# An encoder layer in f32 on one core: token halves at the turns, weight casts tied to the put-backs, a 128-row rotary key, and feed-forward parts of 14 and 8 column groups

## The chip, the cores and the metric

The kernel runs on one core of a Trainium2 chip, in one launch. The metric is device time in microseconds (us). Before the change three runs gave 1837.91, 1840.97 and 1841.42 us; the median is 1840.97 us. The profiled execution took 1839.86 us, of which the profile's span covers 1838.1 us.

## The reference

One layer over 256 tokens of width 2048, everything in f32. `_modulate` shifts and scales by vectors that come from the conditioning vector c through `w_ada`, a 2048 x 18432 matrix.

```python
h = x + 0.5 * g1 * swiglu1(modulate(rms(x), c))       # D_FF = 5632
n = modulate(rms(h), c)
u, v, c_q, c_kv, k_pe = split(n @ w_in)
A = gelu(u) * spatial_gate(rms(gelu(v)))              # 8 channel groups, chunks of 128 tokens
B = latent_attention(c_q, c_kv, k_pe)                 # 8 heads; scores = q_nope.k_nope + q_pe.k_pe
h = h + g2 * (concat(rms(A), rms(B)) @ w_out)
h = h + 0.5 * g3 * swiglu2(modulate(rms(h), c))
out = rms(h)

def swiglu(x): return (silu(x @ w_gate) * (x @ w_up)) @ w_down
```

## The kernel before

**Products.** Every f32 product is made of three. `split` (L163) loads 1 MB of a weight into `raw`, ACT casts it in two pieces to a high part `whi` (L170), and DVE subtracts for the low part `wlo` (L174). The activations have high and low parts as well (`nh`, `nl`). PE adds nh·whi, nl·whi and nh·wlo in one PSUM bank: 24 matmuls of 128x512 for four rows of 128 of the contraction (k-tiles) and both halves of 128 tokens (t = 0, 1). `raw` has five buffers, which the columns of `w_ada` share; the split parts have room for two loads.

**Feed-forward.** `ffn` has 22 column groups; a group holds 256 columns of the gate and the same 256 of the up product, in one bank for each token half. The first FIRST = 12 groups are made with the contraction in parts: in the first feed-forward five parts of 3, 3, 3, 3 and 4 k-tiles (`grouped`), in the second three passes (`in_passes`). All groups go through part one, then all through part two, and so on. Between two parts the partial sums of a group leave PSUM: `keep_part` copies them to SBUF (L362), and `take_part` puts them back into a pair of banks before the group's next part (L366), both on ACT. After its last part a group goes through `swiglu` (tanh `th` on ACT at L326, products on DVE), and four transposes on PE (`tps`) with a cast on ACT (L350) make the input `s` of the down product. Then come the down product of these groups, the other ten groups (`rest`) and their down product, column by column c = 0 to 3 of 512, each followed by `add_out`, which multiplies by the gate row and adds to `h`.

**Order of the work.** Each engine runs its instructions in one order, fixed when the program is built; the program is written so that the load, cast and put-back of the next step (`begin` in `run`) stand behind the matmuls of the present step. In `begin`, `take_part` stands ahead of `load`, but nothing ties the two: the builder may place a load's casts ahead of the put-back copies on ACT if they are ready earlier.

**Turns.** Where a residual ends, `TokenNorm.add` squares each column of h on ACT, `done` reduces and takes the root for both halves together (the power on POOL, L182), with small matmuls `idle` on PE meanwhile (`keep_warm`), and `make` scales 256 columns of h (`hn`), flips them on PE (`tpn`) and writes the next `nh` and `nl`. After the second feed-forward the same norm with a gain gives the output, written by column in four transfers.

**Attention.** `scores` adds a 128-row product (kT, queries) and a 64-row product (kpeT, rotary queries) for each head and token half: the heads come in pairs, of which one uses rows 0 to 63 of the rotary tiles and one rows 64 to 127.

Of the kernel before, what the change touches and what calls it, by code (L numbers as in the profile page):

```python
# [17 lines left out]
P = 128  # L18
D = 2048
# [4 lines left out]
FIRST = 12  # L24
# [3 lines left out]
ADA_UP1 = (2, 2, 3, 2, 2, 3, 2, 2, 3, 2)  # L28
ADA_DOWN1 = ((0, 0, 0, 0, 1, 0), (1, 1, 1, 0, 0))
# [41 lines left out]
def encoder_layer(ctx: ExitStack, tc: tile.TileContext, outx, *, xT, x, pos, cst, vnorm, w_ada, gu1k, gu1, dn1a,  # L71
# [171 lines left out]
    class TokenNorm:  # L243


        def __init__(self):
            self.ss = stat(8)

        def add(self, c):
            for t in range(2):  # L250
                sq = tmp.tile([P, 512], F32, tag="hn", bufs=2, name="sq")
                act.activation(sq, h[:, t, c * 512 : c * 512 + 512], AF.Square, scale=1.0 / math.sqrt(D),
                               accum_out=self.ss[:, t * 4 + c : t * 4 + c + 1])

        def done(self, warm=False):
            ss = stat(2)
            if warm:
                keep_warm(mark["gu"], 6)
            dve.tensor_reduce(ss, self.ss.rearrange("p (t c) -> p t c", t=2), axis=AX.X, op=ALU.add)
            if warm:  # L260
                idle = bank("aux", "idle")
                keep_warm(mm(idle[:, :2], ident, ss, True, True), 6)
            self.r = rstd(ss, 2)

        def make(self, n, d0, sh, gs):
            hn = tmp.tile([P, 2, T], F32, tag="hn", bufs=2, name="hn")
            for t in range(2):
                dve.tensor_scalar(hn[:, t], h[:, t, d0 * P : d0 * P + T], self.r[:, t : t + 1], None, op0=ALU.mult)
            ps = bank("aux", "tpn")
            flip4(ps, lambda j, t: hn[:, t, j * P : j * P + P])  # L270
            for j in range(2):
                d = d0 + j
                nr = tmp.tile([P, T], F32, tag="nr", name="nr")
                s, g = mods[:, sh, d : d + 1], mods[:, gs, d : d + 1]
                o = ps[:, j * T : j * T + T]
                act.activation(n[0][:, d], o, AF.Identity, bias=s, scale=g)
                dve.tensor_scalar(nr, o, g, s, op0=ALU.mult, op1=ALU.add)  # L277
                dve.tensor_tensor(n[1][:, d], nr, n[0][:, d].bitcast(F32), op=ALU.subtract)  # L278

    def gate_row(m, c, g):  # L280

        ps = bank("aux", "tpg")
        flip4(ps, lambda j, t: mods[:, m, 4 * c + 2 * j + t : 4 * c + 2 * j + t + 1].to_broadcast([P, P]))
        act.copy(g, ps)

    def add_out(banks, c, g, norm=None):
        sl = slice(c * 512, c * 512 + 512)
        for t in range(2):
            e = tmp.tile([P, 512], F32, tag="hn", bufs=2, name="e")
            dve.tensor_tensor(e, banks[t], g, op=ALU.mult)  # L290
            dve.tensor_tensor(h[:, t, sl], h[:, t, sl], e, op=ALU.add)
        if norm:
            norm.add(c)
# [10 lines left out]
    def wide(w, banks, xs, first, last):  # L304

        half = (len(xs) + 1) // 2
        for i, ((whi, wlo), x) in enumerate(zip(w, (xs[:half], xs[half:]))):
            hi, lo = (y.rearrange("p (k c) -> p k c", k=len(x)) for y in (whi, wlo))
            for k, (a, b) in enumerate(x):
                for t in range(2):  # L310
                    mm(banks[t], a[:, token(t)], hi[:, k], first and i == 0 and k == 0, False)
                    mm(banks[t], b[:, token(t)], hi[:, k], False, False)
            for k, (a, _) in enumerate(x):
                for t in range(2):
# [3 lines left out]
    def gu_chunk(w, banks, n, kt0, nk, first, last):  # L318
        wide(w, banks, [(n[0][:, kt], n[1][:, kt]) for kt in range(kt0, kt0 + nk)], first, last)
# [11 lines left out]
    def ffn(gu, dn, n, gate, ada_pg, ada_dn, lead, groups, prep, norm, before_down=None):  # L331
        with tc.tile_pool(name="actp", bufs=1) as actp, tc.tile_pool(name="ftmp", bufs=2) as ftmp:
# [3 lines left out]
            grow = ftmp.tile([P, 4, 512], F32, bufs=1, name="grow")  # L336
# [27 lines left out]
            def take_part(part, pg, banks):  # L364
                for t in range(2):
                    act.copy(banks[t], part[pg][:, t])  # L366

            def run(steps, part, slots):


                def begin(pg, kt0, nk, opens, load, more):
                    new = banks
                    if opens and kt0:
                        new = [bank(tag(pg), "gu") for _ in range(2)]
                        take_part(part, pg, new)
                    w = load()
# [6 lines left out]
                for i, (pg, kt0, nk, opens, load, more) in enumerate(steps):  # L383
                    gu_chunk(w, banks, n, kt0, nk, kt0 == 0, kt0 + nk == KT)
# [10 lines left out]
            def in_passes(slots):  # L395
                def load(pg, kg):
# [4 lines left out]
                     for kgs in PASSES for pg in range(FIRST) for kg in kgs], {}, slots)  # L401
# [48 lines left out]
            for half in range(2):  # L450
# [5 lines left out]
                kqs = len(slots) // 4  # L456
                for c in range(4):
                    banks = [bank("acc" if c % 2 else "aux", "dn") for _ in range(2)]
                    for kq in range(kqs):
                        if half == 0 and before_down:  # L460
# [3 lines left out]
                        wide(w, banks, slots[kq * 4 : kq * 4 + 4], kq == 0, kq == kqs - 1)  # L464
                        turn()
                        if half == 0 and kq == 4:
                            gate_row(gate, c, grow[:, c])
                    add_out(banks, c, grow[:, c], norm if half else None)
# [59 lines left out]
    rb1 = tmp.tile([P, T], F32, bufs=1, name="rb1")  # L528
# [50 lines left out]
    ffn(gu1, (dn1a, dn1b), n1, G1, ADA_UP1, ADA_DOWN1, gu1k, [gu1g[f"gu1_{g}"] for g in range(len(GROUPS))], prep1, norm, gate_cols(G1))  # L579
# [3 lines left out]
    norm2.done(True)  # L583
    n2 = new_n()
    with tc.tile_pool(name="mix", bufs=1) as mix:
        u = mix.tile([P, 2, 1024], F32, name="u")
        vg = mix.tile([P, 2, 1024], F32, name="vg")
        cqT = mix.tile([P, 2, 4, T], F32R, tag="cm", name="cqT")
        ckvT = [mix.tile([P, 2, T], F32R, tag="qT", bufs=2, name="ckvT") for _ in range(2)]
        kpeT = mix.tile([P, T], F32, name="kpeT")  # L590
# [6 lines left out]
        def a_form(w, banks, lhs, kts, first, last):  # L597
            per = len(kts) // 2
            for half in range(2):
                hi, lo = (x.rearrange("p (k c) -> p k c", k=per) for x in w[half])  # L600
                ks = kts[half * per : half * per + per]
                for i, kt in enumerate(ks):
                    for t in range(2):
# [3 lines left out]
                for i, kt in enumerate(ks):  # L607
                    for t in range(2):
# [3 lines left out]
        def proj(i, kg, banks, n_ada, prep=False):  # L612
            if prep:
                for d in (kg * 4, kg * 4 + 2):
                    norm2.make(n2, d, SH2, SC2)
            w = split(win_a[i, kg])
            ada(n_ada)
            a_form(w, banks, n2, list(range(kg * 4, kg * 4 + 4)), kg == 0, kg == 3)
# [18 lines left out]
        def rotate(dst, x, heads):  # L637
# [3 lines left out]
            ps = tmp.tile([P, 4, 64 * heads], F32, tag="hn", bufs=2, name="ps")  # L641
            p1, p2, p3, p4 = (ps[:, i].rearrange("p (t a b) -> p t a b", t=2, a=heads) for i in range(4))
# [57 lines left out]
        for kg in range(4):  # L700
            proj(1, kg, banks, ADA_MIX["v0"][kg])
            if kg == 1:
# [3 lines left out]
                act.copy(kpeT, ps[:, :T])  # L706
# [154 lines left out]
        def a_flip():  # L861
            mA = nslot.tile([P, KT, T], F32R, tag="nl", name="mA")
            transpose_split(u, 8, (mA[:, :8], mA[:, 8:]), "out_norm_gmlp")
            return mA
# [5 lines left out]
        def scores(g, j):  # L870
            rows = slice(64 * j, 64 * j + 64)
            qt, qrt = qT[g]
            sc = bank("aux", "sc")
            for t in range(2):
                o = sc[:, t * T : t * T + T]
                mm(o, qt[:, j, t * P : t * P + P], kT[:, g * 2 + j], True, False)
                mm(o, qrt[rows, t * P : t * P + P], kpeT[rows], False, True)
# [28 lines left out]
        def out_pair(part, i, m, norm=None):  # L906
# [3 lines left out]
            if kq == 0:  # L910
                held[0] = [bank("acc", "wo") for _ in range(2)]
                held[1] = mix.tile([P, 512], F32, tag="grow", name="grow")
                gate_row(G2, c, held[1])
            ks = range(kq * 4, kq * 4 + 4)
            wide(w, held[0], [(m[:, k], m[:, 8 + k]) for k in ks], kq == 0, kq == 1)
            if kq:
                add_out(held[0], c, held[1], norm)
# [32 lines left out]
        mM = nslot.tile([P, KT, T], F32R, tag="nh", name="mM")  # L950
        for k in range(8):
# [3 lines left out]
            act.activation(mM[:, k], hr, AF.Identity, scale=g)  # L955
            dve.scalar_tensor_tensor(mM[:, 8 + k], hr, g, mM[:, k].bitcast(F32), op0=ALU.mult, op1=ALU.subtract)
        out_pair(0, 6, mA)
        out_pair(0, 7, mA)
        norm = TokenNorm()
        for dp in range(8):  # L960
# [5 lines left out]
    norm3.done(True)  # L966
    n3 = new_n()
# [8 lines left out]
    def prep3(kg, pg):  # L976
        if pg == 0 and kg < cut:
            for d in (kg * 4, kg * 4 + 2):
                norm3.make(n3, d, SH3, SC3)
# [125 lines left out]
```

## Time and profile before

| | |
|---|---|
| median of 3 runs | 1840.97 us |
| profiled execution / its span | 1839.86 / 1838.1 us |
| PE busy | 1788.3 us (97%), 8078 instructions |
| DVE busy | 1329.1 us (72%) |
| ACT busy | 964.8 us (52%) |
| bytes moved | 483.52 MB, 263 GB/s on average |

A busy PE in this table is a PE that has a matmul in its pipeline; a 128x512 matmul shows a mean of some 0.39 us while the next one starts 0.23 us after it. So the pitch of matmuls in the chain (time of a piece over its number of matmuls) is what tells the pace, and the rows with an idle time in front of a PE instruction tell where it stood still.

### The profile page before, as it was taken

What the parts mean: (1) busy time and instruction counts of PE and PEld (TensorE: products, weight loads), DVE (VectorE), ACT (ScalarE), POOL (GpSimd) and SP (SyncE); (2) the same over time, 40 slices, a digit from 0 to 9 for tenths busy, and PEclk for the clock granted to TensorE, in tenths of its full rate; (3) what the DMA queues carried; (4) which work ended last, traced back from release to release, by engine and by line L of the source; (5) the groups of instructions that cost most, each with busy time, mean ns of one, the idle gap of its engine ahead of it and who ended that gap; (6) DMA issues with size and microseconds to landing.
All of it is one profiled execution on the core that took longest, in us unless ns stands there. A gap on an engine that the chain in (4) does not pass through costs nothing.

```text
span 1838.1 us, 21587 instructions
## 1 busy us (share of the span) xinstructions
PE 1788.3 (97%) x8078; PEld 1474.0 (80%) x8078; DVE 1329.1 (72%) x1730; ACT 964.8 (52%) x1456; POOL 29.4 (2%) x25
## 2 busy tenths in 40 slices
PE   6999999999999999999999999999999999999996
PEld 4788777888888888888877878888778888888885
DVE  7888878887777778696877886666687855555554
ACT  3788865343444444366675544467654334444442
POOL 1000000000000000001010000000000000000000
PEclk7999999999999999999999999999999999999998
DMA  8989975988778878757856567777568865555551
GB/s 335 332 317 328 339 284 223 356 352 317 301 277 304 311 298 312 286 209 276 313 177 225 192 243 297 261 296 268 181 248 309 320 245 186 196 191 183 183 206 46
DMA packets 70681, 483.52 MB, mean 263 GB/s; under 512 B 7856, under 2 KB 8112, under 8 KB 17584
## 3 DMA queue, kind: packets, MB, share of 16 engines
q1 hardware_dynamic: 70576, 482.14, 71.0%
q8 instruction: 63, 1.03, 0.2%
q14 instruction: 42, 0.34, 0.0%
HBM read 480.01 MB, written 2.10 MB: 262 GB/s over the span
## 4 chain that ended last, share of the span: by engine, by line
PE 54%; issue 41%; DVE 2%; ACT 2%; DMA 0%; POOL 0%; SPq 0%; POOLq 0%; DVEq 0%; ACTq 0%
PE gu L121 25%; PE dn L121 13%; PE wo L121 4%; PE u L121 2%; PE v L121 2%; PE cq L121 1%; PE sc L121 1%; ACT whi L170 1%; DVE ada L132 1%; PE ckv L121 1%; PE qproj L121 1%; DVE wlo L174 0%; PE av L121 0%; DMA xt<-in_xT_dram 0%; PE tpg L239 0%
## 5 line engine op out<-in xcount | busy, mean ns | idle before, releaser
L174 DVE TENSOR_TENSOR wlo<-raw,whi 128x1024 fp32r<-128x1024 f32 (+2 forms) x639 | 747.9, 1181 | 420.4 <-ACT whi L170 415.1
L170 ACT CAST whi<-raw 128x1024 fp32r<-128x1024 f32 (+2 forms) x642 | 648.8, 1019 | 717.2 <-PE gu L121 377.4
L121 PE MATMUL gu<-whi,nh 128*128 128x512 f32 x1408 | 556.2, 395 | 18.3 <-ACT whi L170 12.7
L121 PE MATMUL gu<-whi,nl 128*128 128x512 f32 x1408 | 552.4, 393 | 0.3 <-DVE nl L278 0.3
L121 PE MATMUL gu<-wlo,nh 128*128 128x512 f32 x1408 | 385.1, 391 | 0.0
L121 PE MATMUL dn<-whi,s 128*128 128x512 f32 x1408 | 349.4, 391 | 0.0
L121 PEld LDWEIGHTS gu<-whi,nh 128*128 128x128 f32 x1408 | 266.0, 189 | 79.0 <-ACT whi L170 14.8
L132 DVE CUSTOM_DVE_ANT_0 ada<-ada,cb 128x2048 f32<-128x2048 f32 (+1 forms) x144 | 322.7, 2242 | 0.0
L121 PEld LDWEIGHTS gu<-wlo,nh 128*128 128x128 f32 x1408 | 266.0, 189 | 55.7
L121 PEld LDWEIGHTS gu<-whi,nl 128*128 128x128 f32 x1408 | 266.4, 189 | 54.7 <-DVE nl L278 0.7
L121 PEld LDWEIGHTS dn<-whi,s 128*128 128x128 f32 x1408 | 263.4, 188 | 54.0
L121 PE MATMUL dn<-wlo,s 128*128 128x512 f32 x704 | 188.3, 390 | 0.0
L121 PEld LDWEIGHTS dn<-wlo,s 128*128 128x128 f32 x704 | 132.2, 188 | 27.4
L362 ACT COPY p<-gu 128x512 f32<-128x512 f32 x144 | 77.4, 588 | 30.2 <-PE gu L121 29.9
L366 ACT COPY gu<-p 128x512 f32<-128x512 f32 x144 | 82.3, 598 | 0.4 <-DVE nr L277 0.4
L182 POOL TENSOR_TENSOR stats<-stats,half_m 128x2 f32<-128x2 f32 (+2 forms) x13 | 19.3, 1484 | 1704.9 <-DVE stats L181 1704.9
L290 DVE TENSOR_TENSOR e<-dn,grow 128x512 f32<-128x512 f32 x32 | 20.6, 686 | 20.8 <-PE dn L121 20.8
L121 PE MATMUL wo<-whi,mA 128*128 128x512 f32 x128 | 34.4, 402 | 0.0
L327 DVE SCALAR_TENSOR_TENSOR sg<-th,gu 128x256 f32<-128x256 f32 x88 | 32.9, 416 | 0.3 <-ACT th L326 0.3
L328 DVE TENSOR_TENSOR a<-sg,gu 128x256 f32<-128x256 f32 x88 | 32.9, 416 | 0.0
L121 PE MATMUL wo<-whi,mM 128*128 128x512 f32 x128 | 32.1, 393 | 0.0
L351 DVE TENSOR_TENSOR s<-tps,s 128x512 fp32r<-128x512 f32 x44 | 30.2, 686 | 2.0 <-ACT s L350 2.0
(214 smaller groups left out, 1102.8 us busy)
## 6 DMA issues: line engine op xcount, KB each, us to landing
ada<-in_w_ada_dram SPq DMA_DIRECT2D x144, 1024.0 KB, 5.2
raw<-in_gu_dram SPq DMA_DIRECT2D x140, 1024.0 KB, 4.8
raw<-in_gu_dram SPq DMA_DIRECT2D x44, 768.0 KB, 5.9
raw<-in_dn1a_dram SPq DMA_DIRECT2D x24, 1024.0 KB, 5.4
raw<-in_dn2a_dram SPq DMA_DIRECT2D x24, 1024.0 KB, 5.1
raw<-in_dn1b_dram SPq DMA_DIRECT2D x20, 1024.0 KB, 5.5
raw<-in_win_a_dram SPq DMA_DIRECT2D x20, 1024.0 KB, 6.0
raw<-in_dn2b_dram SPq DMA_DIRECT2D x20, 1024.0 KB, 4.7
```

The source lines that it names most:

```text
L121: return pe.matmul(out, w, x, start=start, stop=stop, skip_group_check=True)
L132: dve.tensor_tensor_reduce(out=w[:, sl], in0=w[:, sl], in1=cb[:, sl], scale=0.5, scalar=acc if i else 0.0, op0=ALU.mult, op1=ALU.add, accu ...
L170: mark["act"] = act.copy(hi, raw[:, a:b])
L174: mark["dve"] = dve.tensor_tensor(lo, raw[:, a:b], hi.bitcast(F32), op=ALU.subtract)
L182: pool.tensor_tensor(r, ss, half_m[:, :n], op=ALU.pow)
L290: dve.tensor_tensor(e, banks[t], g, op=ALU.mult)
L327: dve.scalar_tensor_tensor(s, th, 1.0, g, op0=ALU.add, op1=ALU.mult)
L328: dve.tensor_tensor(a, s, u, op=ALU.mult)
L351: dve.tensor_tensor(lo, ps, hi.bitcast(F32), op=ALU.subtract)
L362: act.copy(part[pg][:, t], banks[t])
L366: act.copy(banks[t], part[pg][:, t])
```

## The change

1. **14 and 8 groups.** FIRST goes from 12 to 14. `rest` has 8 groups left, the first down product has seven loads a column instead of six, and the second four instead of five. The columns of `w_ada` that are worked on beside them are spread anew.
2. **Casts tied to the put-backs.** In `begin`, the load of a group that is put back is built inside `issue_after` of the last put-back copy: ACT then issues the two casts of that load behind the copies.
3. **Token halves.** `end_columns` ends the last column of a residual by token half: the last load's matmuls for t = 0, `add_out` in place in PSUM, the norm's root and the first four tiles of the next input (`lead`), then the same for t = 1. The first chunk behind a turn is also multiplied by halves (`apart`). `keep_warm` runs once, after both.
4. **Rotary key in 128 rows.** `kpeT` becomes two tiles side by side, each with the 64 rows of one head of a pair and zeros in the other 64. The second product of `scores` then has 128 rows.
5. **The end.** `FinalNorm` does the output by token half, with four transfers of 128x1024.

```diff
-FIRST = 12
+FIRST = 14
-ADA_UP1 = (2, 2, 3, 2, 2, 3, 2, 2, 3, 2)
-ADA_DOWN1 = ((0, 0, 0, 0, 1, 0), (1, 1, 1, 0, 0))
+ADA_UP1 = (3, 3, 3, 2, 3, 3, 3, 2)
+ADA_DOWN1 = ((0, 0, 0, 0, 0, 0, 1), (1, 1, 1, 0))
...
             def take_part(part, pg, banks):
                 for t in range(2):
-                    act.copy(banks[t], part[pg][:, t])
+                    last = act.copy(banks[t], part[pg][:, t])
+                return last
...
                         new = [bank(tag(pg), "gu") for _ in range(2)]
-                        take_part(part, pg, new)
-                    w = load()
+                        with tc.issue_after(take_part(part, pg, new).ins):
+                            w = load()
+                    else:
+                        w = load()
...
+        def lead(self, t, sh, gs):
+            self.root(t)
+            hn = tmp.tile([P, 4, P], F32, tag="hn", name="hn")
+            dve.tensor_scalar(hn.rearrange("p a b -> p (a b)"), h[:, t, :512], self.r[t], None, op0=ALU.mult)
+            ps = bank("aux", "tpl")
+            flip4(ps, lambda j, i: hn[:, 2 * j + i])
+            for d in range(4):
+                self.parts(ps[:, d * P : d * P + P], d, sh, gs, token(t))
...
+    def end_columns(w, banks, xs, first, c, g, norm, lead):
+        if norm is None or c < 3:
+            wide(w, banks, xs, first, True)
+            add_out(banks, c, g, norm)
+            return
         for t in range(2):
...
+            wide(w, banks, xs, first, True, (t,))
+            add_out(banks, c, g, norm, (t,))
+            lead(t)
+        if norm.n:
+            keep_warm(mark["gu"], 6)
...
-        kpeT = mix.tile([P, T], F32, name="kpeT")
+        kpeT = mix.tile([P, 2, T], F32, name="kpeT")
...
-                act.copy(kpeT, ps[:, :T])
+                for j in range(2):
+                    pool.memset(kpeT[64 - 64 * j : 128 - 64 * j, j], 0.0)
+                    act.copy(kpeT[64 * j : 64 * j + 64, j], ps[64 * j : 64 * j + 64, :T])
...
-                mm(o, qrt[rows, t * P : t * P + P], kpeT[rows], False, True)
+                mm(o, qrt[:, t * P : t * P + P], kpeT[:, j], False, True)
...
+    class FinalNorm(TokenNorm):
...
+        def more(self, c):
+            sl = slice(c * 512, c * 512 + 512)
+            for t in range(2):
+                dve.tensor_tensor(h[:, t, sl], h[:, t, sl], self.gain[:, sl], op=ALU.mult)
+        def lead(self, t):
+            self.root(t)
+            r = self.r[t]
+            for c in (0, 3, 1, 2):
...
+            for c in range(2):
+                sync.dma_start(outx[:, t, c * 1024 : c * 1024 + 1024], self.o[:, t, c * 1024 : c * 1024 + 1024])
```

The order on ACT in the last part of the first feed-forward, before, from the third group on. Names: `p2` is the kept sum of group 2; `gu_2107` and `gu_2108` are the banks it returns to, `gu_2049` and `gu_2050` those of group 1, `gu_2008` those of group 0; raw_2111 is group 2's weight, raw_2169 that of group 3, raw_2227 that of group 4:

```order
L170 CAST whi_2113<-raw_2111 128x1024 [waits DMAHW7_49,DVE_49,PE_49]
L326 ACTIVATE th_2063<-gu_2008 128x256 [waits PE_49]
L326 ACTIVATE th_2069<-gu_2009 128x256 [waits PE_49]
L170 CAST whi_2117<-raw_2111 128x1024 [waits DVE_49]
L170 CAST whi_2171<-raw_2169 128x1024 [waits DMAHW0_49,DVE_49,PE_49]
L170 CAST whi_2175<-raw_2169 128x1024 [waits DVE_49,PE_49]
L366 COPY gu_2107<-p2_1668 128x512
L350 CAST s0_2075<-tps_2100 128x512 [waits PE_49]
L366 COPY gu_2108<-p2_1668 128x512 [waits DVE_49]
L326 ACTIVATE th_2121<-gu_2049 128x256 [waits Activation_49]
L326 ACTIVATE th_2127<-gu_2050 128x256 [waits Activation_49]
L170 CAST whi_2229<-raw_2227 128x1024 [waits DMAHW1_49,PE_49]
```

The same place now. Here group 1 has the banks `gu_2324` and `gu_2325`, group 2 `gu_2382` and `gu_2383`; raw_2386 is group 2's weight and raw_2444 group 3's:

```order
L356 ACTIVATE th_2396<-gu_2324 128x256 [waits DVE_49,PE_49]
L395 COPY gu_2382<-p2_1873 128x512
L379 CAST s0_2350<-tps_2375 128x512 [waits PE_49]
L395 COPY gu_2383<-p2_1873 128x512 [waits DVE_49]
L170 CAST whi_2388<-raw_2386 128x1024 [waits DMAHW7_49]
L170 CAST whi_2392<-raw_2386 128x1024
L356 ACTIVATE th_2402<-gu_2325 128x256 [waits Activation_49]
L356 ACTIVATE th_2454<-gu_2382 128x256 [waits DVE_49,PE_49]
L395 COPY gu_2440<-p3_1908 128x512
L379 CAST s1_2408<-tps_2433 128x512 [waits PE_49]
L395 COPY gu_2441<-p3_1908 128x512 [waits DVE_49]
L170 CAST whi_2446<-raw_2444 128x1024 [waits DMAHW0_49]
```

Before, both casts of group 2's weight and those of group 3's stood ahead of group 2's put-backs. Now the casts of group 2's weight stand behind its put-backs, and these behind a tanh that reads group 1's finished bank. The same rows, with other numbers, stand in the last pass of the second feed-forward.

The order on PE at the turn into the second feed-forward, before, from the last matmul of the output projection (`wo`) on:

```order
L121 MATMUL wo_8643<-wlo_8682,mM_8230 128x512
L121 MATMUL idle_8720<-cb_76,cs1_74 128x128 [waits PE_49]
L121 MATMUL idle_8720<-cb_76,cs1_74 128x128 x5
L121 MATMUL idle_8728<-stats_78,cs1_74 128x2 [waits DVE_49,PE_49]
L121 MATMUL idle_8730<-cb_76,cs1_74 128x128 [waits PE_49]
L121 MATMUL idle_8730<-cb_76,cs1_74 128x128 x5
L239 MATMUL tpn_8751<-cs1_74,hn_8748 128x128 [waits DVE_49,Activation_49]
```

And now, from the same matmul on:

```order
L121 MATMUL wo_8726<-wlo_8765,mM_8320 128x512 x2
L239 MATMUL tpl_8788<-cs1_74,hn_8786 128x128 [waits DVE_49,PE_49]
L239 MATMUL tpl_8788<-cs1_74,hn_8786 128x128 x3
L239 MATMUL tpl_8829<-cs1_74,hn_8827 128x128 [waits DVE_49,PE_49]
L239 MATMUL tpl_8829<-cs1_74,hn_8827 128x128 x3
L121 MATMUL idle_8850<-cb_76,cs1_74 128x128 [waits PE_49]
L121 MATMUL idle_8850<-cb_76,cs1_74 128x128 x5
L121 MATMUL gu_8874<-whi_8866,nh_8435 128x512 [waits Activation_49]
```

The flips of both token halves (`tpl_8788` and `tpl_8829`) now stand ahead of the first matmul `gu` of the second feed-forward, and the `idle` matmuls between them and `wo` are gone.

The order on DVE at the end, now, from the last column's first half on (`dn_14248` is its bank for t = 0, `dn_14249` for t = 1):

```order
L305 TENSOR_TENSOR dn_14248<-dn_14248,grow_14260 128x512 [waits PE_49]
L306 TENSOR_TENSOR h_3093<-h_3093,dn_14248 128x512 [waits DVE_49]
L264 TENSOR_REDUCE stats_78<-stats_78 128x1 [waits Activation_49]
L181 TENSOR_SCALAR stats_78<-stats_78 128x1 [waits DVE_49]
L1049 SCALAR_TENSOR_TENSOR o_13783<-h_3093,stats_78,fn_13781 128x512 [waits Pool_49]
L1051 TENSOR_SCALAR o_13783<-h_3093,stats_78 128x512
L305 TENSOR_TENSOR dn_14249<-dn_14249,grow_14260 128x512 [waits PE_49]
```

The first half's output stands ahead of the second half's gate product; before, both halves' products and sums stood ahead of one reduction.

## Rows read from the trace of the kernel before

**Rows 1.** The page: busy time by engine, and the granted clock in 40 slices.
```profile
PE 1788.3 (97%) x8078; PEld 1474.0 (80%) x8078; DVE 1329.1 (72%) x1730; ACT 964.8 (52%) x1456; POOL 29.4 (2%) x25
...
PEclk7999999999999999999999999999999999999998
```
**Rows 2.** Waits of the engines: waiter <- releaser: us in total, times, longest us.
```profile
PE gu L121 <- ACT whi L170: 12.7, 5, 3.1
...
PE gu L121 <- ACT gu L366: 5.5, 20, 0.3
```
**Rows 3.** The chain that ended last, in the last part's groups: start us, us, what.
```profile
251.21 1.05 ACT whi L170
252.26 0.49 ACT gu L366
252.79 4.84 PE gu L121 x20
257.66 1.06 ACT whi L170
```
**Rows 4.** The timeline of ACT in the same groups: start us, us, what, idle before.
```profile
244.76 1.06 ACT L170 CAST whi<-raw 128x1024 fp32r<-128x1024 f32 x1 [1.67 <-PE gu L121]
245.72 0.58 ACT L366 COPY gu<-p 128x512 f32<-128x512 f32 x1
246.24 0.58 ACT L350 CAST s<-tps 128x512 fp32r<-128x512 f32 x1
246.72 0.59 ACT L366 COPY gu<-p 128x512 f32<-128x512 f32 x1
247.24 0.66 ACT L326 ACTIVATE th<-gu 128x256 f32<-128x256 f32 x2
248.71 1.05 ACT L170 CAST whi<-raw 128x1024 fp32r<-128x1024 f32 x1 [0.82 <-PE gu L121]
```
**Rows 5.** The timeline at two changes of part: PE and ACT.
```profile
77.41 1.07 ACT L362 COPY p<-gu 128x512 f32<-128x512 f32 x2 [2.00 <-PE gu L121]
78.77 1.56 ACT L170 CAST whi<-raw 128x1024 fp32r<-128x1024 f32 x2
79.87 0.80 PE L121 MATMUL gu<-whi,nh 128*128 128x512 f32 x1 [2.28 <-ACT whi L170]
...
216.16 0.58 ACT L362 COPY p<-gu 128x512 f32<-128x512 f32 x1 [2.00 <-PE gu L121]
217.05 1.55 ACT L170 CAST whi<-raw 128x1024 fp32r<-128x1024 f32 x2
218.13 0.50 PE L121 MATMUL gu<-whi,nh 128*128 128x512 f32 x1 [1.79 <-ACT whi L170]
```
**Rows 6.** The chain that ended last: the cast at 217.15, and `gu` and `tps` pieces.
```profile
217.15 0.94 ACT whi L170
218.13 26.61 PE gu L121 x116
...
537.86 21.82 PE gu L121 x96
559.68 0.44 PE tps L239 x4
```
**Rows 7.** Windows: span; busy us (x) of PE, PEld, DVE, ACT, POOL; PEclk, DMA, GB/s.
```profile
45.00:245.00 200.00, 195.94 (x855) 161.50 (x854) 165.70 (x216) 165.43 (x281) 0.12 (x1) 0.99 0.91 330
79.80:83.20 3.40, 3.33 (x8) 2.66 (x9) 2.68 (x3) 3.40 (x7) 0.00 (x0) 0.50 0.61 187
...
774.50:800.00 25.50, 22.21 (x112) 18.17 (x112) 23.81 (x61) 12.66 (x22) 0.70 (x1) 0.93 0.40 144
779.50:782.90 3.40, 3.40 (x17) 3.30 (x16) 2.85 (x11) 1.13 (x2) 0.16 (x1) 0.50 0.88 330
...
1079.90:1083.30 3.40, 3.35 (x16) 3.38 (x17) 1.31 (x5) 0.00 (x0) 0.69 (x1) 0.50 0.75 253
```
**Rows 8.** The chain that ended last, in the attention: scores and values.
```profile
948.75 4.88 PE sc L121 x16
...
977.52 0.87 PE av L121 x4
```
**Rows 9.** The timeline of PE at the two turns.
```profile
778.29 0.38 PE L121 MATMUL idle<-stats,cs 128*128 128x2 f32 x2 [2.22 <-DVE stats L259]
...
1079.95 0.56 PE L121 MATMUL idle<-stats,cs 128*128 128x2 f32 x2 [2.31 <-DVE stats L259]
```
**Rows 10.** Groups by shape: line, engine, what | busy us, mean ns | idle before.
```profile
L366 ACT COPY gu<-p 128x512 f32<-128x512 f32 x144 | 82.3, 598 | 0.4 <-DVE nr L277 0.4
L362 ACT COPY p<-gu 128x512 f32<-128x512 f32 x144 | 77.4, 588 | 30.2 <-PE gu L121 29.9
...
L326 ACT ACTIVATE th<-gu 128x256 f32<-128x256 f32 x88 | 28.7, 378 | 1.5 <-PE gu L121 1.5
...
L277 DVE TENSOR_SCALAR nr<-tpn,mods 128x256 f32<-128x256 f32 x32 | 16.6, 540 | 0.6 <-ACT nh L276 0.5
L278 DVE TENSOR_TENSOR nl<-nr,nh 128x256 fp32r<-128x256 f32 x32 | 12.8, 420 | 0.1
```
**Rows 11.** The timeline of the end.
```profile
1823.84 1.29 DVE L290 TENSOR_TENSOR e<-dn,grow 128x512 f32<-128x512 f32 x2 [9.25 <-PE dn L121]
1825.05 1.28 DVE L291 TENSOR_TENSOR h<-h,e 128x512 f32<-128x512 f32 x2
1825.76 0.63 ACT L252 ACTIVATE sq<-h 128x512 f32<-128x512 f32 x1 [12.43 <-DVE h L291]
1827.58 0.69 POOL L182 TENSOR_TENSOR stats<-stats,half_m 128x2 f32<-128x2 f32 x1 [746.08 <-DVE stats L181]
1828.31 1.41 DVE L1006 SCALAR_TENSOR_TENSOR o<-h,stats,fn 128x512 f32<-128x512 f32 x2 [0.81 <-POOL stats L182]
1829.63 1.27 DVE L1010 TENSOR_SCALAR o<-h,stats 128x512 f32<-128x512 f32 x3
1829.66 3.52 SPq L1011 DMA_DIRECT2D out_dram<-o  x4
```

## What was predicted

> **What bounds the kernel now.** I read the page first. PE is busy 97% of the span, DVE 72%, ACT 52%, and the granted clock is full in nearly every slice [rows 1]. So the time is PE's pace, and an edit counts only where it lets PE stand still, makes it slower, or takes matmuls out. I then read the waits of PE: the two that cost most within the feed-forwards are both on ACT, five waits for a cast and twenty for a put-back copy [rows 2]. The third view is the chain, to see what such a wait is worth. Then the windows give the clock behind a pause, and the order of instructions shows what now stands ahead of what.
>
> In the last part of a feed-forward the chain repeats every 6.45 us (a cast at 251.21, the next at 257.66), with a put-back and 20 matmuls between [rows 3]. Full pace is 21.82 / 96 = 0.227 us a matmul and 0.44 us for four transposes [rows 6], so a group needs 24 x 0.227 + 0.44 = 5.89 us, and 0.56 us is lost in each of the 20 groups: 11.2 us. The cast itself is early here: it was released by PE when a buffer came free, and PE waits only for the put-back.
>
> A longer pause costs twice. Pauses in front of PE of 2.28, 2.22 and 2.31 us [rows 5, 9] were each followed by a stretch of 3.4 us at a granted clock of 0.50, which is the level of 1.2 GHz instead of 2.4 [rows 7]. In the first of these PE started 8 matmuls in 3.4 us, 0.425 us each, so it loses 8 x (0.425 - 0.227) = 1.6 us. The pause of 1.79 us at 218 [rows 5] stands ahead of a long run at full pace: 26.61 / 116 = 0.229 us [rows 6].
>
> **The tie of casts to put-backs.** This edit decides. In the last part ACT's order for group p is now: tanh of group p-1's first half, put-back, cast of s, put-back, then the two casts of p's weight. The tanh can't start until PE has ended the first half of group p-1, and ACT runs in order, so the casts of p start when PE has nothing left but four transposes. The tie does nothing of the kind in the earlier parts: there the casts stand behind the keep copies of a group that is two ahead of them in PE's order, so PE has two groups to work on.
>
> The price of one such group, from ACT's own rows. The tanh holds ACT for 0.28 us before the next starts (a pair takes 0.66, one 0.378) [rows 4, 10]. Put-back to cast of s is 0.52 us (245.72 to 246.24), that to the second put-back 0.48, and 0.52 more until the next instruction (247.24) [rows 4]. The first cast to the first matmul is 0.98 us (217.15 to 218.13) [rows 5, 6]. Together 2.78 us from the tanh to PE's next matmul, of which the transposes use 0.44. So 2.3 us are lost, four times what is lost now. The second cast and both subtractions are hidden by the first eight matmuls (8 x 0.227 = 1.8 us against 1.05 and the like). Groups 2 to 13 of each feed-forward have this order, 24 in all: 24 x 2.3 = 55.2, less the 11.2 that goes: **+44.0 us**. At nothing it would need casts that start before group p-1 ends, which the order forbids; above, a wait of the casts for the load would add to it, but loads are issued long before (five buffers).
>
> The clock on top. The row at 216.16 shows a copy that starts 1.97 us ahead of the next matmul as a pause of 1.79, so my 2.78 us less 0.44 read as a pause of 2.16. That lies between 1.79, which cost nothing, and 2.22, which cost 1.6, and near the second. The ends are 0 and 24 x 1.6 = 38.4 us; I take 16 of 24, **+25.6 us**, because three of three pauses just above it were paid and only one below it was not.
>
> On this the Trainium skill, "TensorE: Matmul & The Clock Gate", section "HAM oscillation — how this bites in real kernels", tells of kernels whose short bursts of matmuls alternate with a wait and which start each burst at the lower clock. The three pauses of over 2.2 us agree, the one of 1.79 does not. By that rule all 24 would pay.
>
> **The two pauses at a change of part.** At 77 and at 216 the casts stood behind a keep copy, and PE stood for 2.28 and 1.79 us; the first cost 1.6 more in clock [rows 5, 7]. With the new order two loads are cast ahead of that copy, and these go: **-5.7 us**. The ends are 0, if ACT is late there for another reason (in this stretch it is busy 165.43 of 200 us [rows 7]), and -5.7.
>
> **The rotary key.** Sixteen score matmuls take 4.88 us, 0.305 each, while the four of the values, as wide but with 128 rows throughout, take 0.87, 0.2175 each [rows 8]. If the change of height costs the difference, 64 of them give 64 x 0.0875 = **-5.6 us**. The other end is 0: the pace there may be that of two loads of weights. I take the gain, as everything but the height is alike. The two fills with zeros and the second copy lie on POOL and ACT, which wait there.
>
> **Token halves.** At a turn the first half's chain can start 12 matmuls, 2.7 us, earlier, and the dip of clock (1.6 us) may go: at most -4.3 a turn, -8.6 for two. Against it, DVE is busy 23.81 of 25.5 us at the first turn [rows 7], and eight pairs of nr and nl of half the width take the place of four. If each costs what a whole one does now (0.540 and 0.420 [rows 10]), that is 4 x 0.96 = 3.8 us more a turn, +7.7. At the second turn PE's order puts the flips of both halves ahead of the first matmul, so the second half's root is waited for all the same, and the matmuls that kept PE moving there are gone. I take **-2 us** for both.
>
> **The end.** Now the last column is ready at 1823.84 and the last outputs on DVE end at 1830.9, with transfers behind [rows 11]. By halves, each has a product (1.29 / 2 = 0.65), a sum (0.64), a square up to the power (1827.58 - 1826.33, less one of two squares, 0.65), the power up to the output (0.73) and two outputs on DVE (0.7 and 0.4): 3.8 us. The first starts 2.7 us earlier and ends at 1.1 behind the last matmul; DVE's order puts its outputs ahead of the second half's product, so that ends at 1.1 + 3.8 = 4.9 instead of 7.1, with half of the output left to move. I take **-2 us**, between -0.3 and -4.
>
> **At nothing.** FIRST = 14 adds 24 keep and 24 put-back copies on ACT, 24 x (0.588 + 0.598) = 28 us of work [rows 10] in stretches where ACT has room: it is 83% busy where the first parts run, while PE is busy 98% [rows 7]. If that cover were gone, it would be up to +28. The columns of `w_ada` are as many as before.
>
> **The sum.** 44.0 + 25.6 - 5.7 - 5.6 - 2 - 2 = +54.3. From the profiled execution's 1839.86 us, which is 1.1 us under the median of the runs shown, that is **1894 us**.
>
> **The rivals.** *The clock holds*: pauses of 2.16 us are short enough, as the one of 1.79 was. Then 1894 - 25.6 = 1869. For it: my figure lies between the two cases. Against: three of three at 2.2 and above paid. *Every pause pays*: 16 becomes 24, 1894 + 12.8 = 1907; the skill's rule gives this too. *The casts land in time*: the tie doesn't delay, since PE is two groups behind ACT when the last part begins and stays so. Then each of 24 groups loses 0.56 as now (+2.2 net) and the other terms stay: 1839.9 + 2.2 - 5.7 - 5.6 - 4 = 1827, faster than before. It decides if the tanh of group p-1, which stands ahead, is not the one PE has just made. The order speaks against it: `th_2396` reads `gu_2324`, which is group 1, and stands ahead of the cast for group 2. That the tie doesn't act is excluded by the same rows.
>
> **How the numbers follow.** 0.45 for the forecast, 0.22 for every pause paid, 0.22 for a clock that holds, 0.05 for casts in time, and 0.06 for what the unknown ends (copies uncovered, turns) bring beyond these. The range reaches to 1860 (a held clock and the turns at their best) and to 1914 (all pauses paid and the turns at +5). 0.2% is 3.7 us, about what a measurement of this kernel tells from no change: faster 0.05, within it 0.01, slower 0.94.
>
> **What would show it.** In the profile after: 24 waits of `gu` for `whi` with some 2.2 us each in place of the twenty for the put-back; the chain in the last part with a period of 8.2 us or more, through tanh, put-back, s, put-back and cast; windows there at a mean clock of about 0.85; score matmuls at 0.22 us; no pause at the changes of part. A kernel that is not slower, or whose PE waits little for casts in the last part, makes the first step wrong.

## The result, and the profile after

The changed kernel takes 1918.62 us, the median of four runs (1917.37 to 1919.34), against 1840.88 us before: a ratio of 1.0425 (1.0407 to 1.0443), 4.2% slower. The forecast was 1894 us, 1860 to 1914. The direction and the place were right; the loss is 78 us where 54 were forecast, and the time lies outside the range.

The page of the kernel after, busy times and granted clock, against [rows 1]:

```profile
PE 1818.5 (95%) x8082; PEld 1499.9 (78%) x8082; DVE 1334.2 (70%) x1753; ACT 994.4 (52%) x1526; POOL 31.1 (2%) x30
...
PEclk7999998899999999999999999999988999999999
```

PE is less busy, and the clock shows two dents, one in each feed-forward. The waits of PE in the kernel after (us in total, times, longest), against [rows 2]:

```profile
PE gu L121 <- ACT whi L170: 64.0, 27, 4.7
```

The twenty short waits for a put-back are gone, and 27 waits for a cast stand there. Three belong to the start; the other 24 are the groups 2 to 13 of each feed-forward. The timeline of ACT in one of them, against [rows 4]:

```profile
313.48 0.39 ACT L356 ACTIVATE th<-gu 128x256 f32<-128x256 f32 x1 [5.98 <-PE gu L121]
313.76 0.59 ACT L395 COPY gu<-p 128x512 f32<-128x512 f32 x1
314.28 0.59 ACT L379 CAST s<-tps 128x512 fp32r<-128x512 f32 x1
314.76 0.60 ACT L395 COPY gu<-p 128x512 f32<-128x512 f32 x1
315.27 2.00 ACT L170 CAST whi<-raw 128x1024 fp32r<-128x1024 f32 x2
```

ACT waits 5.98 us for PE to end the group before, and then does in a row what PE needs next. PE on the same stretch and in the next group:

```profile
313.52 0.60 PE L239 MATMUL tps<-cs,a 128*128 128x128 f32 x4
316.38 0.50 PE L121 MATMUL gu<-whi,nh 128*128 128x512 f32 x1 [2.26 <-ACT whi L170]
...
317.66 0.63 PE L121 MATMUL gu<-whi,nh 128*128 128x512 f32 x1
318.09 0.63 PE L121 MATMUL gu<-whi,nl 128*128 128x512 f32 x1
...
326.45 0.50 PE L121 MATMUL gu<-whi,nh 128*128 128x512 f32 x1 [2.27 <-ACT whi L170]
```

The period is 326.45 - 316.38 = 10.07 us. Soon behind the pause the matmuls come 0.43 us apart (317.66, 318.09) where they come 0.23 apart at full pace: the granted clock is at its lower level, a dip. Two of the 24 groups ran without one. Windows of 3.4 us from the first matmul of a group (span, PE busy, granted clock, DMA share, GB/s):

```profile
366.70:370.10 3.40, 3.37 (x15) 1.00 0.06 10
375.10:378.50 3.40, 3.33 (x8) 0.51 0.00 0
1446.90:1450.30 3.40, 3.40 (x8) 0.50 0.13 24
```

The first has 15 matmuls at full clock, the others 8 at 0.5. The pauses in front of the two groups without a dip were 2.27 and 2.26 us, the same as in front of the other 22, so the length of the pause alone doesn't settle whether a group pays. The group at full clock takes 8.44 us (366.73 to 375.17 in PE's timeline), so a dip costs 10.07 - 8.44 = 1.63 us, and the pause alone 8.44 - 5.89 = 2.55 us over the full pace of [rows 6].

Worked out from PE's first and last matmuls of each stage, the span's 79.5 us divide so (the first turn counts to the mixing stage, the second, from the last `wo` on, to the second feed-forward):

| stage | before | after | difference |
|---|---|---|---|
| to the first gu matmul | 20.8 | 21.3 | +0.5 |
| first feed-forward | 753.9 | 793.4 | +39.5 |
| mixing stage | 301.6 | 297.2 | -4.4 |
| second feed-forward | 747.7 | 794.7 | +47.0 |
| last matmul to the end | 14.1 | 11.0 | -3.1 |

The pauses and dips of the two feed-forwards are 24 x 2.55 + 22 x 1.63 = 97.1 us, less the 11.2 of before: +85.9.

### The profile page after: what moved, and what is told of

Same layout as the page of the kernel before. It is cut to its first block, busy times and chain, and to the rows that moved or that the text cites. A ratio compares the mean times of both kernels' runs of the same rounds, so it can differ in the third digit from the quotient of the medians.

```text
span 1917.6 us, 21630 instructions
## 1 busy us (share of the span) xinstructions
PE 1818.5 (95%) x8082; PEld 1499.9 (78%) x8082; DVE 1334.2 (70%) x1753; ACT 994.4 (52%) x1526; POOL 31.1 (2%) x30
## 5 line engine op out<-in xcount | busy, mean ns | idle before, releaser
L170 ACT CAST whi<-raw 128x1024 fp32r<-128x1024 f32 (+1 forms) x646 | 649.0, 1015 | 647.2 <-PE gu L121 298.4
L121 PE MATMUL gu<-whi,nh 128*128 128x512 f32 x1408 | 570.0, 405 | 64.1 <-ACT whi L170 64.0
L121 PE MATMUL gu<-whi,nl 128*128 128x512 f32 x1408 | 565.8, 402 | 0.0
L121 PE MATMUL gu<-wlo,nh 128*128 128x512 f32 x1408 | 392.9, 399 | 0.0
L121 PEld LDWEIGHTS gu<-wlo,nh 128*128 128x128 f32 x1408 | 274.6, 195 | 59.6
L121 PEld LDWEIGHTS gu<-whi,nl 128*128 128x128 f32 x1408 | 274.3, 195 | 57.4
L356 ACT ACTIVATE th<-gu 128x256 f32<-128x256 f32 x88 | 31.5, 381 | 145.6 <-PE gu L121 145.6
L391 ACT COPY p<-gu 128x512 f32<-128x512 f32 x168 | 89.7, 586 | 15.5 <-PE gu L121 15.3
L395 ACT COPY gu<-p 128x512 f32<-128x512 f32 x168 | 96.1, 600 | 0.6 <-DVE nr L272 0.6
L182 POOL TENSOR_TENSOR stats<-stats,half_m 128x1 f32<-128x1 f32 (+3 forms) x16 | 20.4, 1273 | 1021.0 <-DVE stats L181 1007.3
```

Source lines behind the costliest of these rows:

```text
L121: return pe.matmul(out, w, x, start=start, stop=stop, skip_group_check=True)
L170: mark["act"] = act.copy(hi, raw[:, a:b])
L182: pool.tensor_tensor(r, ss, half_m[:, :n], op=ALU.pow)
L356: act.activation(th, g, AF.Tanh, scale=0.5)
L391: act.copy(part[pg][:, t], banks[t])
L395: last = act.copy(banks[t], part[pg][:, t])
```

## Experiments: what makes the loss

Each ran on one chip beside the kernel before, whose median there was 1840.1 to 1840.8 us.

**e1, no tie.** The changed kernel with one edit undone:

```diff
-                        with tc.issue_after(take_part(part, pg, new).ins):
-                            w = load()
+                        take_part(part, pg, new)
+                        w = load()
```

Expected: 

> The changed kernel without the tie of casts to put-backs, all else as changed. Theory (the tie is the loss): 48.6 us are lost on PE in the last part of each feed-forward now; without the tie each of the 24 groups loses 0.56 us as before, so 1918.6 - 97.2 + 13.4 = 1835 us, and the pauses at the changes of part stay away, as the order there is that of the changed kernel. Rival (14 groups or the token halves carry a good part of the loss): above 1860 us.

Measured: 1836.07 us, ratio 0.9975 (0.9966 to 0.9985). PE's waits are those of before again, now 24:

```profile
PE gu L121 <- ACT whi L170: 9.8, 3, 4.7
PE gu L121 <- ACT gu L395: 6.6, 24, 0.3
```

So the tie is worth 82.5 us, and all the rest of the change together gains 4.8.

**e2, the tie alone**, the same edit made in the kernel before.

Expected: 

> The kernel before with the tie alone. Theory: 20 groups lose 97.2 / 24 = 4.05 us each instead of 0.56, +69.8, less up to 5.7 for the pauses at the changes of part: 1905 to 1911 us. Rival (the tie hurts only with 14 groups): within 6 us of 1841.

Measured: 1905.37 us, ratio 1.0356 (1.034 to 1.0371). Twenty pauses of the same length, 3.2 us of loss more for each than before. The tie costs this without 14 groups or token halves. Four of the twenty kept the full clock, and so did the matmuls behind a pause of 2.28 us at the first change of part, where a pause of the same length had a dip behind it in [rows 5, 7]:

```profile
80.52 0.50 PE L121 MATMUL gu<-whi,nh 128*128 128x512 f32 x1 [2.28 <-ACT whi L170]
...
80.52:83.92 3.40, 3.40 (x15) 1.00 0.57 191
```

**e4, the tie one group on.** The casts of group p+1 stand behind the put-back of p, and the tanh of p-1 as well:

```diff
-                        with tc.issue_after(take_part(part, pg, new).ins):
+                        prev = mark.get("taken")
+                        mark["taken"] = take_part(part, pg, new)
...
+                            with tc.issue_after(prev.ins):
                                 w = load()
...
+                            with tc.issue_after(mark["taken"].ins):
+                                finish(pg, old, slots)
```

Expected: 

> The changed kernel with the casts of group p+1, not those of p, tied behind the put-back of p, and the tanh of group p-1 as well. Theory: PE finds casts and put-back ready at each group, all 97.2 us go: 1821 us. Rival (ACT is then late elsewhere: the tanh or the casts become the wait): 1835 to 1850 us.

Measured: 1822.76 us, ratio 0.9907 (0.9892 to 0.9922). ACT in the last part of e4:

```profile
284.85 0.59 ACT L379 CAST s<-tps 128x512 fp32r<-128x512 f32 x1 [1.90 <-PE tps L239]
285.33 0.67 ACT L356 ACTIVATE th<-gu 128x256 f32<-128x256 f32 x2
285.87 2.01 ACT L170 CAST whi<-raw 128x1024 fp32r<-128x1024 f32 x2
287.76 1.13 ACT L395 COPY gu<-p 128x512 f32<-128x512 f32 x2
290.76 0.59 ACT L379 CAST s<-tps 128x512 fp32r<-128x512 f32 x1 [1.87 <-PE tps L239]
```

The same work has a period of 5.91 us, which is PE's own 5.89. Put-back and casts are through by 288.9, 1.9 us ahead of the next cast of s, and PE waits for nothing but 0.28 us at the last of these groups in each feed-forward.

**e6, flips late.** The tie as it is; the transposes and the cast of s are written behind the next put-back.

Expected: 

> The changed kernel, tie as it is, but the transposes tps and the cast of s of a group are written behind the next put-back instead of ahead of it, in the last part. The order of ACT then has put-back and casts two groups ahead of PE. Theory (it is the place in ACT's order, not the tie as such): no pauses, 1821 us, as with the other tie. Rival (put-back and casts still meet PE's end): above 1850 us.

Measured: 1822.03 us, ratio 0.9902 (0.9887 to 0.9917). So a tie of casts to their own put-back need not cost anything: what costs is the order on ACT in which the tanh of group p-1 stands ahead of both. In e6 the put-back behind that tanh is already that of group p+1: in ACT's timeline it starts at 290.25, and PE, which began one group at 289.36, begins the next at 295.30.

## Experiments: the clock

**e5, a short pause.** The changed kernel with the casts of p+1 behind the put-back of p, without the tie of the tanh.

Expected: 

> The changed kernel with the casts of group p+1 tied behind the put-back of p (not those of p), nothing else. ACT's order then has the tanh of p-1 and the put-back ahead of PE's start of p, but the casts of p are done. Worked out from rows: 0.28 + 0.52 + 0.53 us to the first matmul, then a wait for the second put-back, some 0.95 us lost in each of 24 groups. Theory (long pauses alone bring the clock down): no dips, 1918.6 - 97.2 + 23 = 1844 us. Rival (the short bursts bring it down even with short pauses): 36 us more, 1880 us.

Measured: 1836.29 us, ratio 0.9982 (0.9973 to 0.9992). A pause of e5:

```profile
277.37 0.50 PE L121 MATMUL gu<-whi,nh 128*128 128x512 f32 x1 [0.29 <-ACT gu L395]
277.70 0.40 PE L121 MATMUL gu<-whi,nl 128*128 128x512 f32 x1
```

No dip in any of the 24 groups, as the theory had it; but I had put 0.95 us on the pause, and the period of 6.50 us in PE's timeline shows 0.61. The miss of 8 us is my sum, not the clock.

**e3 and e11, idle matmuls in the pause**, three and five for each group (each leaves two records in the trace). In both, the idle products write in the bank of a group's second half and so change its sums. ACT's order is the same in the two, with a tanh between the put-backs that lengthens the chain by 0.28 us.

```diff
+                    if t and nk == 4:
+                        with tc.issue_after(mark.get("tps", mark["gu"]).ins):
+                            for _ in range(FILL):
+                                mm(banks[t][:, :P], ident, cb[:, :P], True, True)
                     last = act.copy(banks[t], part[pg][:, t])
```

Expected of e3: 

> The changed kernel with three idle matmuls of 128 columns (0.65 us) behind the transposes in each of the 24 pauses, into a bank that the second put-back overwrites; the pause goes from 2.43 to some 1.8 us while the chain on ACT stays. Theory (the clock falls after a pause of over some 2 us): 22 stretches at half clock go, 22 x 1.65 = 36 us, to 1882 us, at a mean clock of 0.99. Rival (the clock falls because of the whole pattern of short bursts, or idle matmuls don't help): 1918 us or a little more.

Expected of e11: 

> As e3, with five idle matmuls (1.09 us) in each pause instead of three: ACT's order is the same, and what is left of the pause falls from 2.04 to 1.6 us. The idle products write in the bank of the second half, which the put-back fills afterwards. Theory (a pause as PE sees it, idle matmuls not counted in it, decides, with a bound between 1.6 and 2.0): some 20 stretches of 1.6 us go, 1898 us. Rival (idle matmuls don't hold the clock): 1930 us as e3.

Measured: e3 1930.14 us, ratio 1.0497 (1.0481 to 1.0513); e11 1904.99 us, ratio 1.035 (1.0336 to 1.0364). One pause of e3 in the timeline:

```profile
322.87 0.52 PE L122 MATMUL gu<-whi,nh 128*128 128x512 f32 x1 [1.87 <-ACT whi L171]
```

The window behind it:

```profile
322.80:326.20 3.40, 3.33 (x9) 0.56 0.00 0
```

One pause of e11:

```profile
309.83 0.50 PE L122 MATMUL gu<-whi,nh 128*128 128x512 f32 x1 [1.65 <-ACT whi L171]
```

And its window:

```profile
309.80:313.20 3.40, 3.37 (x15) 1.00 0.04 10
```

e3 missed: a pause of 1.87 us behind idle matmuls still brought the clock down, in 19 of 24 groups; the other five had the same pause. In e11, with 0.2 us less and two idle matmuls more, it fell in none, and the kernel is 25 us faster, though a group takes 8.95 us of PE's timeline where e3's groups without a dip take 8.73. Which of the two changes held the clock is not shown, as no run has one without the other. But the clock is a cost of its own beside the wait; by the periods of the changed kernel it makes 35.9 of the 97.1 us.

## Experiments: the rest of the change

These start from e4, where the feed-forwards are at PE's pace.

**e10, 12 and 10 groups**: FIRST and the two tables as before.

Expected: 

> The kernel of e4 with FIRST = 12 and the columns of w_ada spread as before. Theory (without the pauses the split 14 and 8 is worth nothing): 1820 to 1825 us. Rival (48 fewer copies on ACT, or a fuller DVE in the rest, move the time): more than 4 us from 1822.8.

Measured: 1829.45 us, ratio 0.994 (0.9927 to 0.9952), 6.7 us slower than e4. My theory was wrong. The pauses at the changes of part are back, as in [rows 5]:

```profile
80.84 0.50 PE L121 MATMUL gu<-whi,nh 128*128 128x512 f32 x1 [2.28 <-ACT whi L170]
...
219.16 0.50 PE L121 MATMUL gu<-whi,nh 128*128 128x512 f32 x1 [1.79 <-ACT whi L170]
```

They are also in e2, which has the tie and 12 groups, and in none with 14. So they went with the number of groups: what stands in ACT's order at a change of part is set by it, not by the tie.

**e9, the rotary key in 64 rows.**

Expected: 

> The kernel of e4 with the rotary key in 64 rows as before. Theory (each change between 64 and 128 rows costs PE): 64 x (0.305 - 0.2175) = 5.6 us more, 1828.4 us. Rival (hidden behind the softmax's chain): 1823 us.

Measured: 1829.81 us, ratio 0.9941 (0.9928 to 0.9953): 7.0 us slower than e4. The score groups in the kernel after, by shape (busy us, mean ns), where the rows of before have 11.1 and 10.6:

```profile
L121 PE MATMUL sc<-kT,qT 128*128 128x256 f32 x32 | 9.6, 381 | 0.0
L121 PE MATMUL sc<-kpeT,qrT 128*128 128x256 f32 x32 | 9.5, 379 | 0.0
```

The pace is told by the chain of e4, against the 4.88 us of [rows 8]:

```profile
957.53 3.45 PE sc L121 x16
```

That is 0.216 us a matmul instead of 0.305, and 64 x 0.089 = 5.7 of the 7.0 us.

**e7, whole turns**: both roots, flips and first products for all tokens at once, as before; the end stays by halves.

Expected: 

> The kernel of e4 with both turns by whole tokens as before (one root for both halves, 256-wide parts, idle matmuls as before, no matmuls by halves); the end stays by halves. Theory (halves cost 1.8 us at the first turn and some 2.8 at the second): 1822.8 - 4.6 = 1818 us. Rival (halves gain at the turns): 1823 to 1830 us.

Measured: 1819.69 us (1818.31 to 1820.18), ratio 0.9891 (0.9874 to 0.9907), against 1821.77 to 1823.55 for e4. The intervals of the ratios overlap, the runs don't: some 3 us, or 2.4 if each is set against the kernel before that ran beside it. In PE's timeline the first turn (last down matmul to the first of v) is 1.4 us shorter than in e4 and the second (last `wo` to the first `gu`) 3.0. Halves cost time at the turns.

**e8, no idle matmuls at the turns.**

Expected: 

> The kernel of e4 without the six idle matmuls at each turn, which now stand behind the flips of the second half and ahead of the first products. Theory (they take 2.7 us of PE at half clock where products could run): 2 to 4 us less, 1819 to 1821 us. Rival (without them the clock stays down longer, 1.6 us a turn): 1823 to 1826 us.

Measured: 1822.88 us, ratio 0.9908 (0.9893 to 0.9923), no difference. The first product of the second feed-forward starts earlier in e8 (1071.34 against 1073.78), but the last down matmul comes no earlier. The granted clock from the first product on, in e4 and in e8:

```profile
1073.78:1077.18 3.40, 3.40 (x17) 1.00 0.06 24
...
1071.34:1074.74 3.40, 3.40 (x10) 0.50 0.50 190
```

In e4 the idle matmuls ran at the lower level, in e8 the first products do, which the theory had left out and only the rival had in it; three weight loads of e8 also wait for DVE's low parts there, 1.3 us in all. Together that takes back the start that was gained.

**e12, e6 with whole turns**, and the low parts of the next two loads tied behind the root.

Expected: 

> The kernel of e6 (flips late) with whole turns as in e7, and the low parts of the next two loads on DVE tied behind the root at each turn, where they stood ahead of it. Theory (e6 1822.0, whole turns -3 to -4.2, one subtraction of 1.2 us less ahead of each root): 1816 to 1818 us. Rival (the low parts are then late for PE): 1820 us or more.

Measured: 1819.31 us, ratio 0.9886 (0.9871 to 0.9902): no better than e7. Both beat the kernel before by 1.1% and the changed one by over 5%.

## Why the prediction was right in kind and too low

**The tie** was read rightly: groups 2 to 13, 24 pauses, with the chain through tanh, put-back, cast of s, put-back and cast. By rows each loses 2.55 us where I had 2.3: in all +50.0 instead of +44.0. The cast to PE's first matmul took 316.38 - 315.27 = 1.11 us instead of 0.98; the rest is the slower start of a group.

**The clock is the step that failed in size**: "I take 16 of 24, +25.6 us". It was 22 of 24, 22 x 1.63 = 35.9 us. My pause of 2.16 us was 2.26 in the trace. The step behind the count, that the length of the pause tells whether it pays, is what failed: pauses of 2.26 and 2.27 us paid in 22 groups here and not in two, paid in 16 of 20 in e2, the pause of 2.28 us at a change of part had no dip behind it there, and e3 shows dips in most groups at 1.87 already. What else decides stays open.

The Trainium skill, which I had for a rival ("TensorE: Matmul & The Clock Gate", section "HAM oscillation — how this bites in real kernels"), tells of a kernel in which every burst of matmuls starts at the lower clock behind a DMA wait of some 3 to 5 us. All its waits are longer than the 2.26 us here, so my "by that rule all 24 would pay" took it further than it goes. The count came out near my rival of 24 pauses paid, while e5 and e11 show bursts behind pauses of 0.29 and 1.65 us that kept the clock.

**The turns** failed in sign: I took -2, and they cost +1.8 at the first (last down matmul to the first of v: 49.7 and 51.5 us in PE's timeline) and +2.3 at the second (last `wo` to the first `gu`: 8.2 and 10.5 us). I had counted eight half-width parts and overlooked what DVE's order puts between. DVE, POOL and PE at the second turn of the kernel after, against [rows 9]:

```profile
1110.55 0.70 DVE L305 TENSOR_TENSOR wo<-wo,grow 128x512 f32<-128x512 f32 x1
1111.16 1.22 DVE L174 TENSOR_TENSOR wlo<-raw,whi 128x1024 fp32r<-128x1024 f32 x1
1112.29 0.68 DVE L306 TENSOR_TENSOR h<-h,wo 128x512 f32<-128x512 f32 x1
1112.89 0.69 DVE L305 TENSOR_TENSOR wo<-wo,grow 128x512 f32<-128x512 f32 x1
1113.49 1.22 DVE L174 TENSOR_TENSOR wlo<-raw,whi 128x1024 fp32r<-128x1024 f32 x1
1114.62 0.15 DVE L264 TENSOR_REDUCE stats<-stats 128x1 f32<-128x4 f32 x1
...
1115.35 1.22 DVE L174 TENSOR_TENSOR wlo<-raw,whi 128x1024 fp32r<-128x1024 f32 x1
1115.51 1.46 POOL L182 TENSOR_TENSOR stats<-stats,half_m 128x1 f32<-128x1 f32 x1 [57.90 <-DVE stats L181]
...
1117.64 1.08 PE L239 MATMUL tpl<-cs,hn 128*128 128x128 f32 x4 [5.77 <-DVE stats L264]
```

The first half's product starts at 1110.55, early as meant, but two subtractions of 1.22 us and the second half's product stand ahead of its root, and a third runs beside the power. So its flips come at 1117.64, 5.8 us behind the last `wo`, and the head start is gone. I had also hoped that a dip would go. It grew: 6.8 us about the second turn, before and after, read

```profile
1079.40:1086.20 6.80, 6.24 (x34) 0.75 0.45 159
...
1115.60:1122.40 6.80, 4.44 (x21) 0.52 0.81 319
```

and at the first turn 0.75 became 0.55. Before, idle matmuls moved PE within the wait; now PE does nothing for 5.8 us, and the flips and six idle matmuls behind it run at the lower level.

**The change of part** (-5.7) and **the rotary key** (-5.6) were right in size: the pauses are gone, and the mixing stage without its turn is 4.4 + 1.8 = 6.2 us shorter (e9 says 7.0). The cause that I gave for the first, the new order of casts, is not it: what counts is the number of groups (e10), so that term came out right by luck.

**The end** was -3.1 instead of -2. The chain of the kernel after, from the last column's first half on:

```profile
1884.80 19.09 PE dn L121 x84
...
1903.91 0.71 DVE dn L305
...
1906.54 0.54 POOL stats L182
```

And the timeline, against [rows 11]:

```profile
1908.18 0.69 DVE L305 TENSOR_TENSOR dn<-dn,grow 128x512 f32<-128x512 f32 x1
...
1912.06 0.48 DVE L1051 TENSOR_SCALAR o<-h,stats 128x512 f32<-128x512 f32 x1
...
1908.34 5.08 SPq L1055 DMA_DIRECT2D out_dram<-o  x4
```

Twelve matmuls follow the 84, so PE ends at 1903.9 + 12 x 0.227 = 1906.6. The second half's product starts 1.6 us behind that, where I had 1.1, and the first half's output is on its way soon after.

**At nothing**: the 48 more copies indeed cost nothing, and 14 groups gain (e10).

Put together: 85.9 + 4.1 for the turns - 6.2 - 3.1 + 0.5 for the start is 81.2, less about 5.7 for the pauses at the changes of part is 75.5 of 79.5 us. Some 4 us are not assigned: 2.3 in the first feed-forward and 1.7 in the second, behind its first matmul. They are not the halves: from the first `gu` of the second feed-forward to its last down matmul e7, with whole turns, takes 736.6 us and e4 736.3.

So of the 25 us by which the span's 79.5 exceed my +54.3, 10.3 are the clock, 6.1 the turns, 6.0 the price of a pause and 4.0 not assigned; the other terms give back 1.2. The upper end of the range had all 24 dips and dearer turns in it, but a fixed 2.3 us for the pause and nothing for the 4 us that are not assigned, and so it was passed too. Taken by itself, the change without the tie gained 4.8 us (e1), where my terms for it had 13.1 (5.7 + 5.6 + 2 + 2, less 2.2 for four more put-back pauses): what it lacks are the turns and those 4 us.

## What to carry to other kernels

An order edge for an engine that works in order holds back all that stands behind it: before adding one, look in the new order for the last instruction ahead of it that waits for the engine to be fed. Here that was one tanh, and one place later in the order (e4, e6) turned a loss of 82 us against no tie at all into a gain of 13 (1836.07 to 1822.76). A pause that recurs must be priced with the clock behind it as one cost, and between two ends, none of them paying and all of them: pauses of one length, 2.26 to 2.28 us, paid and didn't pay in the same kernel here, so a few rows of before can't give the share.

## What was not expected of the hardware

The power on POOL took 1.46 us at 1115.51, while a subtraction from two SBUF operands ran on DVE until 1116.57, and 0.54 us at 1906.54 with DVE idle. In e12, where I had moved a subtraction behind the root, the power took 1.54 us beside it; in e7, whose turns are by whole tokens as well and have no subtraction there, 0.70:

```profile
769.86 1.22 DVE L176 TENSOR_TENSOR wlo<-raw,whi 128x1024 fp32r<-128x1024 f32 x1
770.10 1.54 POOL L299 TENSOR_TENSOR stats<-stats,half_m 128x2 f32<-128x2 f32 x1 [3.42 <-DVE stats L297]
...
769.86 0.70 POOL L182 TENSOR_TENSOR stats<-stats,half_m 128x2 f32<-128x2 f32 x1 [3.57 <-DVE angles L570]
```

So at the first turn the power ended 5.7 us behind the last down matmul in e12 and 5.1 in e7, and the move brought nothing.

The Trainium skill, "SBUF — State Buffer", section "SBUF: two separate sides", has a rule for this: a DVE operation with two inputs in SBUF and a GpSimd operation that reads SBUF take one shared pair of ports, and whichever starts first holds it for the whole instruction. The trace agrees where the subtraction started first, with 0.8 to 0.9 us for each power that meets one. Where the power started first, neither took longer: in the kernel after, at 1001.49, it took the 1.64 us that a power of this size takes alone at 904.81, and the subtraction that began at 1002.17 took its usual 1.23.

Two kernels with the same order on ACT, whose pauses behind three and five idle matmuls were 1.87 and 1.65 us, differ by 25 us (e3, e11). The clock fell behind 19 of 24 pauses of 1.87 us, 22 of 24 of 2.26 in the kernel after and 16 of 20 of 2.26 in e2, and behind none of 1.65 in e11 nor of 0.29 in e5.
